# Norm rows from a broadcast column, and the residual added by an accumulating DMA, in a hybrid transformer layer

## The chip, the core and the metric

The kernel runs on one core of one Trainium2 chip. A core has a matrix engine (TensorE, PE in the profile, with its weight loads shown apart as PEld), three engines for element-wise work (VectorE or DVE, ScalarE or ACT, GpSimd or POOL), and SyncE (SP), which here only issues DMAs. Each engine works through its own queue in order, and so a waiting instruction holds up all that is queued behind it. PE reads its operands from the on-chip memory SBUF and writes its results to PSUM, from where DVE or ACT must take them. The metric is the device time of one execution in microseconds (us); the figure for a kernel is the median of several executions.

## The reference, cut to what matters

One layer on x of 1024 tokens by 1024 features, all in float32. Four blocks follow one another, each between two RMS norms, with the residual added after the second:

```
h = h + 0.5 * rmsnorm(swiglu(rmsnorm(h, ffn1_pre_g)), ffn1_post_g)
h = h + rmsnorm(hybrid_mixer(rmsnorm(h, mix_pre_g)), mix_post_g)
h = h + rmsnorm(memory_cross_attention(rmsnorm(h, xa_pre_g), rmsnorm(mem, mem_g)), xa_post_g)
h = h + 0.5 * rmsnorm(swiglu(rmsnorm(h, ffn2_pre_g)), ffn2_post_g)

def rmsnorm(x, g):
    return x * rsqrt(mean(x * x, axis=-1) + 1e-6) * g
```

The mixer joins 16 heads of stick-breaking attention with a Mamba-2 scan (SSD); cross-attention has 4 heads on 256 memory tokens; the feed-forwards have 2816 hidden features.

## The kernel before, in words

Activations lie transposed: features on the 128 partitions, tokens along the free axis. The residual stream h is eight feature tiles (d = 0 to 7) for each of two halves of 512 tokens (hh = 0, 1), so a tile is 128 x 512 float32, 256 KB. To keep float32 accuracy at the speed of the reduced-precision type float32r, each operand is split into a high and a low part (`split`, line 262, and `scaled_split`, line 268: the high part by a cast on ACT, the low part by a subtraction on DVE), and each product is made of three matmuls (`mm3`, line 277): high by high, high by low, low by high. Weights come in over SP's queue and are split on the way (`wtile`, line 174); weights that are needed twice are split once and their parts stored by DMAs on POOL's queue (`khi`, `klo`, line 194). The matrix products of the feed-forwards are done in seven products in place of eight (Strassen's way), `seven` (line 782) and `down_first` (line 1007).

The program is laid out for PE. Every matmul and transpose passes through `_pe` (line 100), which chains it to the one before, so PE's order is the order of the program. `_pe` also keeps a clock: it adds up a cost for each product, some 0.42 ns per column of 512-column products and 213 ns for float32r products of fewer than 256 columns (`mm`, line 130). Other work is entered in a list `later` with a due time on that clock and is issued by `run_later` (line 122) once PE's program has come that far. A norm's products can instead be floating and pinned at a time (`pinned`, line 144). Instructions issued from the list keep the program's order on their engines (`kp`).

A norm has two steps. `rms_cols` (line 317) takes the sum of squares over features: DVE and ACT add up the squares of the eight tiles into one tile `acc` (`sumsq`, line 374), eight small products with a column of 1/1024 bring the mean per token into a column of one bank (tokens on the partitions, four columns for 512 tokens), and ACT and DVE turn it into 1/sqrt. `rms_rows` (line 341) turns these four columns into one tile in which every partition holds the 512 factors as a row, since features lie on the partitions where the factor is to be applied. It splits the columns into `ch` and `cl` (lines 347 and 348), DVE multiplies an identity with each of them into 128 x 512 diagonal tiles (line 358, into `dg` and a low tile that shares its place with the row to be made), and PE sums each over the partitions by a product with a matrix of ones (line 367); ACT copies the result out (line 369). With `behind=True` the products are issued apart from the column's steps. Nineteen rows are made in all, one of them 256 wide.

`post` (line 407) is the second norm of a block, with the residual and the first norm of the next block. For a half it issues `cols` (the column), `rows` (the row), and for each d `apply`: DVE scales the tile F by gain and row (line 428), DVE adds the old h (line 432), POOL issues the store of the new h to memory (line 437), and ACT and DVE split it for the next block (lines 270 and 272 by `scaled_split`). `presum` squares the new tile, and at the end come the next norm's column and row (`tail`). The old h has been loaded for this by `resid` (line 396): eight DMAs on POOL's queue (line 403), each with a due time, into the places of `XL`, the low parts of the operands. There are six such post norms: two in the first feed-forward's down products (`down_first`, lines 1114 and 1136), two in the mixer's output (`mix_out`, lines 2074 and 2078), two in cross-attention (`xattn`, lines 2204 and 2241; the last is issued at once, without due times). The second feed-forward ends otherwise (`down_seven`, `rows_end`) and has its own use of `resid` (lines 1199 and 1200).

In cross-attention (line 2081), the steps of one slice (transposing the softmax values, products with the memory values, results split into the o tiles `oh` and `ol`) alternate with the next slice's scores and, merged by cost, with the projection of a later slice's queries. `place` (line 81) sets aside a given number of bytes per partition so that the tiles behind it lie elsewhere; line 2137 does this ahead of the transposed softmax values and the o tiles. The loads of the keys and values (line 2093) are on POOL's queue.

Here, in the kernel before, are the lines of the row product and of one part:

```
        def product():
            ps = self.norm_bank()
            for i, x in enumerate(parts):
                self.mm(ps[:, 0 : nb * P], self.onesr, x.rearrange("p a b -> p (a b)"), i == 0, i == 1)
```

Of the kernel before, what the change touches and what calls it, by code (L numbers as in the profile page):

```python
# [18 lines left out]
P = 128  # L19
S = 1024  # L20
H = 512
# [25 lines left out]
class Kern:  # L47
# [82 lines left out]
    def mm(self, out, lhsT, rhs, start, stop):  # L130
        n = 1
        for d in out.shape[1:]:
            n *= d
        dt = rhs.dtype
        cost = n * 0.422 * (4 if dt == F32 else 1)
        if dt == F32R and n < 256:
            cost = 213.0
        self._pe(self.nc.tensor.matmul(out, lhsT, rhs, start=start, stop=stop, skip_group_check=self.more), cost)  # L138
# [202 lines left out]
    def rms_rows(self, c, home, behind=False):  # L341

        nc = self.nc
        nb = c.shape[1]
        cs = self.t(self.tp, [P, 16], F32R, "cs", bufs=1)
        ch, cl = cs[:, 0:nb], cs[:, 4 : 4 + nb]
        self.kp(nc.vector.tensor_copy(ch, c))
        self.kp(nc.vector.tensor_tensor(out=cl, in0=c, in1=ch.bitcast(F32), op=ALU.subtract))
        dg = self.t(self.tp, [P, 4, P], F32R, "dg", bufs=1)
        if isinstance(home, tuple):  # L350
            pool, tag = home
            low = self.t(pool, [P, 4, P], F32R, tag, bufs=1)[:, 0:nb, :]
        else:
            low = dg[:, nb : 2 * nb, :]
        parts = dg[:, 0:nb, :], low
        for o, x in zip(parts, (ch, cl)):
            self.kp(
                nc.vector.tensor_tensor(
                    out=o, in0=self.ident[:, :].unsqueeze(1).to_broadcast([P, nb, P]),
                    in1=x.bitcast(F32).unsqueeze(2).to_broadcast([P, nb, P]), op=ALU.mult,  # L360
                )
            )

        def product():
            ps = self.norm_bank()
            for i, x in enumerate(parts):
                self.mm(ps[:, 0 : nb * P], self.onesr, x.rearrange("p a b -> p (a b)"), i == 0, i == 1)
            r = self.t(pool, [P, H], F32, tag, bufs=1) if isinstance(home, tuple) else home
            self.kp(nc.scalar.copy(r, ps[:, 0 : nb * P]))
            return r  # L370

        return product if behind else product()
# [34 lines left out]
    def post(self, hh, gname, r2, gnext=None, out=None, step=None, spread=True, pins=(23000, 28000), accs=None, tail=None, times=None):  # L407
# [17 lines left out]
        def apply(d):  # L425
# [6 lines left out]
            self.kp(nc.vector.tensor_tensor(out=F, in0=F, in1=self.XL[hh][d], op=ALU.add))  # L432
            if out is not None:
                nc.sync.dma_start(out=out[d], in_=F)
                return
# [4 lines left out]
        if out is None:  # L440
            self.h[hh] = [self.tc.dram_tile([P, H], F32, name=self.nm(f"h{hh}{d}")) for d in range(KT)]
# [8 lines left out]
        if step is None:  # L450
# [4 lines left out]
            for d in range(KT):  # L455
                apply(d)
# [6 lines left out]
        for d in range(KT):  # L463
            t = t3 + step * d
            q.append((t, lambda d=d: apply(d)))
            if out is None:
                q.append((t + 800, lambda d=d: presum(d)))
        if out is None:
            c2 = self.t(self.rp, [P, 4], F32, f"cpre{hh}", bufs=2)
            nxt = {}  # L470
            t1, t2 = tail or (t1 + 4000, t2 + 4000)
            self.posted = T0 + t + 900
            q.append((t + t1, lambda: self.rms_cols([accs2], c2)))
            if spread:
                def tail_rows():
                    nxt["r"] = self.rms_rows(c2[:, :], (self.rp, f"rpre{hh}"))
                    if "to" in nxt:
                        self.R[nxt["to"]] = nxt["r"]

                q.append((t + t2, tail_rows))  # L480
            self.next_norm = (nxt, c2)
# [525 lines left out]
    def down_first(self, sp, rw, wdn, act_d, gpost, gnext):  # L1007
# [98 lines left out]
        self.resid(0, 2700, 22000)  # L1106
# [7 lines left out]
        self.post(0, gpost, self.C[0], gnext, step=4700, accs=accs[0], times=(12000, 15500, 17500), tail=(5500, 9000))  # L1114
# [6 lines left out]
        self.resid(1, 2700, 10000)  # L1121
# [14 lines left out]
        self.post(1, gpost, self.C[1], gnext, step=2400, accs=accs[1], times=(4500, 9500, 11500), tail=(13500, 19000))  # L1136
# [854 lines left out]
    def mix_out(self):  # L1991
# [3 lines left out]
        with self.pools("mo", ["r", "a"], ["b"]) as (rp, sp, sp2, dnp):  # L1995
# [44 lines left out]
            self.resid(0, 5000, 12000)  # L2040
            self.run_all(self.first)
            for n, (hh, part) in enumerate(passes):
# [29 lines left out]
                if n == 1:  # L2072
                    self.run_later(float("inf"))
                    self.post(0, "mix_post_g", None, "xa_pre_g", step=5000, spread=False, tail=(18000, 0))
                    self.resid(1, 5000, 17000)
                if n == 3:
                    self.flush(0)
                    self.post(1, "mix_post_g", None, "xa_pre_g", step=3000, spread=False, tail=(22000, 0))


    def xattn(self):
# [3 lines left out]
        with self.pools("xf", ["a", "b"], []) as (sp, sp2, pp):  # L2085
# [158 lines left out]
    def run(self):  # L2244
        nc, tc, ap = self.nc, self.tc, self.ap
        with tc.tile_pool(name="const", bufs=1) as cp, tc.tile_pool(name="state", bufs=1, reuse_waits="tile") as xp, \
# [14 lines left out]
            self.ident = self.t(cp, [P, P], F32, "ident")  # L2261
# [161 lines left out]
```

## Time and profile before

| | |
|---|---|
| time, median of 3 executions | 2641.63 us (2639.55 to 2644.81) |
| the profiled execution | 2645.18 us, its span 2643.4 us |
| granted TensorE clock, mean | 0.992 |
| idle time of PE over the span | 66.5 us |
| DMA | 528.87 MB, mean 200 GB/s |

The profile is of one execution. Its page gives the busy time of each engine; idle time of an engine that is not the bottleneck costs nothing by itself. Matmuls are pipelined, so a matmul's own duration (some 390 ns for 512 columns) is longer than the step from one start to the next (some 0.23 us). A line of the trace names the engine, the line of the kernel that issued the instruction (for products mostly that of a helper, 138), the operation, and the tiles as output, an arrow, and inputs; the buffer's number is left out. "xN" is the count. In the view of waits a line gives the waiting instruction, who released it, the total time in us, the number of times and the longest. In the view of windows each engine has its busy time in that stretch and the number of its instructions, and then follow the granted clock of TensorE as a share of the full one, the DMA engines' busy share and their GB/s. In the view of one line of code, durations are given as minimum, median and maximum in ns, and for DMAs the time from issue to landing in us. In the timeline a row begins with its start in us from the span's beginning and its length, and ends in brackets with the idle time of the engine before it and what ended it.

By stages, in us from the span's start: first feed-forward to about 690, SSD to about 1030, attention to about 1610 (the first output products begin within it), mixer output to about 1740, cross-attention to about 1980, second feed-forward to the end.

### The profile page before, as it was taken

To read this page: it belongs to the slowest core of one execution; us is meant where nothing else is said; L and a number is where in the kernel's file an instruction comes from. 1 tells how busy PE (TensorE), PEld (TensorE's weight loads), DVE (VectorE), ACT (ScalarE), POOL (GpSimd) and SP (SyncE) were. 2 spreads that over 40 slices of the span, in tenths; PEclk is the share of its full clock that TensorE was granted. 3 is DMA by queue.
4 is the path that set the end of the run, shared out by engine and by line. 5 is a ranking of instruction groups with operands and counts; after the bars stand their busy time and mean duration, and the time that the engine had idled before them with its cause. 6 is when DMAs were issued, how large, how long until landed. Compare 5 with 4: busy or idle time off the path is not lost.

```text
span 2643.4 us, 36454 instructions
## 1 busy us (share of the span) xinstructions
PE 2576.9 (97%) x12598; PEld 2135.0 (81%) x12598; DVE 1983.2 (75%) x3085; ACT 1262.9 (48%) x2276; POOL 530.8 (20%) x660
## 2 busy tenths in 40 slices
PE   8999999999999999999999998999999999999998
PEld 6788888887777778888888787887878788888887
DVE  7888787888678774777777777775448989895675
ACT  7544443545367783445554445254445433333432
POOL 1555552001100000000000001122012555542000
PEclk9999999999999999999999999999999999999999
DMA  5688887754721226433434458777667455555976
GB/s 209 238 308 302 304 282 252 255 193 158 259 79 45 71 70 196 115 99 108 109 108 115 146 178 323 252 274 252 218 230 272 167 187 203 195 180 210 347 276 218
DMA packets 225241, 528.87 MB, mean 200 GB/s; under 512 B 28064, under 2 KB 35104, under 8 KB 225056
## 3 DMA queue, kind: packets, MB, share of 16 engines
q1 hardware_dynamic: 190432, 419.56, 48.2%
q0 software_dynamic: 27424, 93.87, 9.8%
q10 hardware_dynamic: 7200, 13.11, 1.3%
q8 instruction: 99, 1.62, 0.3%
q14 instruction: 86, 0.70, 0.1%
HBM read 353.41 MB, written 152.04 MB: 191 GB/s over the span
## 4 chain that ended last, share of the span: by engine, by line
PE 79%; DVE 9%; DMA 6%; ACT 3%; issue 2%; POOL 1%; SPq 0%; DVEq 0%; ACTq 0%; POOLq 0%
PE mm L138 45%; PE dn L138 24%; PE z L138 2%; PE ms L138 2%; PE tr L141 2%; PE y L138 1%; PE ms L141 1%; DMA wraw<-act 1%; DMA raw<-act 1%; DVE hl L265 1%; DVE wlo L265 1%; PE seg L138 1%; DMA blk<-h 1%; DVE whi L265 0%; DMA oraw<-mix 0%
## 5 line engine op out<-in xcount | busy, mean ns | idle before, releaser
L138 PE MATMUL mm<-xh,whi 128*128 128x512 f32 x1288 | 511.5, 406 | 11.1 <-ACT xh L270 7.0
L138 PE MATMUL mm<-xh,wlo 128*128 128x512 f32 x1240 | 478.5, 393 | 3.2 <-DVE wlo L265 2.9
L138 PE MATMUL mm<-xl,whi 128*128 128x512 f32 x1188 | 467.8, 394 | 1.0 <-DVE xl L265 0.7
L138 PEld LDWEIGHTS mm<-xh,whi 128*128 128x128 f32 x1288 | 244.1, 189 | 53.6 <-ACT xh L270 6.9
L138 PEld LDWEIGHTS mm<-xh,wlo 128*128 128x128 f32 x1240 | 234.3, 189 | 55.3 <-DVE wlo L265 3.4
L138 PEld LDWEIGHTS mm<-xl,whi 128*128 128x128 f32 x1188 | 225.6, 190 | 34.1 <-DVE xl L265 1.8
L1823 DVE TENSOR_TENSOR_SCAN nb<-nb,begin 128x128 f32<-128x128 f32 (+7 forms) x128 | 171.7, 1352 | 55.0 <-ACT nb L1819 54.4
L1819 ACT ACTIVATE nb<-z,scale 128x128 f32<-128x128 f32 (+2 forms) x192 | 107.8, 580 | 88.8 <-PE z L138 87.7
L263 ACT CAST whi<-wraw 128x1024 fp32r<-128x1024 f32 (+1 forms) x89 | 81.2, 914 | 69.1 <-PE mm L138 39.1
L1856 POOL MEMSET ath<- 128x128 f32 x64 | 13.1, 205 | 499.0 <-PE mm L138 499.0
L265 DVE TENSOR_TENSOR wlo<-wraw,whi 128x1024 fp32r<-128x1024 f32 x61 | 74.4, 1220 | 38.3 <-ACT whi L263 38.0
L138 PE MATMUL dn<-xh,wlo 128*128 128x512 f32 x296 | 101.0, 389 | 0.0
L737 POOL TENSOR_TENSOR wc<-wraw,raw 128x512 f32<-128x512 f32 x57 | 87.5, 1535 | 66.6 <-DVE whi L265 30.7
L737 POOL TENSOR_TENSOR wc<-raw,wraw 128x512 f32<-128x512 f32 x55 | 85.5, 1555 | 66.5 <-DVE wlo L265 31.4
L819 POOL TENSOR_TENSOR ft<-ft,e 128x512 f32<-128x512 f32 x38 | 62.4, 1642 | 144.2 <-DVE e L818 85.7
L650 ACT ACTIVATE ft<-ft 128x512 f32<-128x512 f32 x88 | 55.4, 631 | 75.0 <-DVE ft L649 70.3
L263 ACT CAST ath<-tr 128x512 fp32r<-128x512 f32 (+1 forms) x107 | 58.2, 545 | 67.5 <-PE tr L141 66.1
L138 PE MATMUL dn<-xh,blk 128*128 128x512 f32 x280 | 90.2, 389 | 0.0
L265 DVE TENSOR_TENSOR atl<-tr,ath 128x512 fp32r<-128x512 f32 (+1 forms) x107 | 67.0, 629 | 29.2 <-ACT ath L263 28.9
L138 PE MATMUL dn<-xh,whi 128*128 128x512 f32 x256 | 88.0, 389 | 0.0
L138 PE MATMUL mm<-ath,v 128*128 128x256 f32 x320 | 86.2, 291 | 0.6 <-DVE sq L1838 0.6
L382 DVE TENSOR_TENSOR acc<-acc,sq 128x512 f32<-128x512 f32 x78 | 52.3, 684 | 42.5 <-ACT sq L381 42.2
(586 smaller groups left out, 6667.9 us busy)
## 6 DMA issues: line engine op xcount, KB each, us to landing
whi<-dwhi SPq DMA_DIRECT2D x57, 512.0 KB, 3.4
wlo<-dwlo SPq DMA_DIRECT2D x57, 512.0 KB, 4.2
wraw<-act SPq DMA_DIRECT2D x102, 256.0 KB, 4.4
raw<-act SPq DMA_DIRECT2D x96, 256.0 KB, 4.3
wraw<-in_w_gu SPq DMA_DIRECT2D x44, 512.0 KB, 4.4
raw<-in_w_gu SPq DMA_DIRECT2D x38, 512.0 KB, 4.8
khi<-whi POOLq DMA_DIRECT2D x30, 512.0 KB, 4.6
klo<-wlo POOLq DMA_DIRECT2D x30, 512.0 KB, 6.7
```

Of the source, the lines that this page charges most:

```text
L138: self._pe(self.nc.tensor.matmul(out, lhsT, rhs, start=start, stop=stop, skip_group_check=self.more), cost)
L141: self._pe(self.nc.tensor.transpose(out, src, self.ident if ident is None else ident), 109.0)
L263: self.kp(self.nc.scalar.copy(hi, src))
L265: (eng or self.nc.vector).tensor_tensor(out=lo, in0=src, in1=hi.bitcast(F32), op=ALU.subtract)
L382: self.kp(nc.vector.tensor_tensor(out=accs[i % 2], in0=accs[i % 2], in1=sq, op=ALU.add))
L650: nc.scalar.activation(t, t, AF.Silu)
L737: nc.gpsimd.tensor_tensor(out=t, in0=a, in1=b, op=op)
L819: nc.gpsimd.tensor_tensor(out=t1, in0=t1, in1=e, op=ALU.mult)
L1819: nc.scalar.activation(nb[:, s0:s1], z[:, 0:n], AF.Sigmoid, scale=sc[:, i : i + 1])
L1823: nc.vector.tensor_tensor_scan(out=nb[:, 0:Wd][:, ::-1], data0=nb[:, 0:Wd][:, ::-1], data1=begin[:, S - Wd : S][:, ::-1], initial=0.0, op0 ...
L1856: nc.gpsimd.memset(x[:, 0, :].bitcast(F32), 0.0)
```

## The change

Four edits, as the diff has them:

- The row product has no diagonal tiles any more. The four columns themselves, each broadcast along the free axis, are the weights of products with the identity as the moving operand, 128 columns each; two (high and low) for each of four columns, eight in all, each with a cost of 80 on the planner's clock. The identity tile is now of type float32r, and its float32 view serves the transposes.
- `post` no longer uses loaded copies of h. The part is divided: `scale` (the DVE scaling, then a DMA on POOL's queue that adds the old h from memory into F), and `lag` later `apply` (the store of the new h, the split). The loads by `resid` ahead of the six post norms are gone; the second feed-forward keeps its own.
- The due times change: in the first feed-forward, first half, column, row and first part go from 12000, 15500, 17500 to 16500, 18500, 20500, the step from 4700 to 3700, and the next norm from 5500 and 9000 behind the last part to 3500 and 6500; in the others so that the last `apply` falls due at about the same time as before.
- The place ahead of the o tiles in cross-attention grows from 128 to 384 bytes per partition.

```diff
-        dg = self.t(self.tp, [P, 4, P], F32R, "dg", bufs=1)
-        if isinstance(home, tuple):
-            pool, tag = home
-            low = self.t(pool, [P, 4, P], F32R, tag, bufs=1)[:, 0:nb, :]
-        else:
-            low = dg[:, nb : 2 * nb, :]
-        parts = dg[:, 0:nb, :], low
-        for o, x in zip(parts, (ch, cl)):
-            self.kp(
-                nc.vector.tensor_tensor(
-                    out=o, in0=self.ident[:, :].unsqueeze(1).to_broadcast([P, nb, P]),
-                    in1=x.bitcast(F32).unsqueeze(2).to_broadcast([P, nb, P]), op=ALU.mult,
-                )
-            )
+        pool, tag = home if isinstance(home, tuple) else (None, None)
 
         def product():
             ps = self.norm_bank()
-            for i, x in enumerate(parts):
-                self.mm(ps[:, 0 : nb * P], self.onesr, x.rearrange("p a b -> p (a b)"), i == 0, i == 1)
-            r = self.t(pool, [P, H], F32, tag, bufs=1) if isinstance(home, tuple) else home
+            for b in range(nb):
+                for i, x in enumerate((ch, cl)):
+                    self.mm(
+                        ps[:, b * P : (b + 1) * P], x[:, b : b + 1].to_broadcast([P, P]), self.identr,
+                        i == 0, i == 1, 80.0,
+                    )
+            r = self.t(pool, [P, H], F32, tag, bufs=1) if pool else home
...
+        before = self.h[hh]
+
+        def scale(d):
             F = self.F[hh][d]
             self.kp(
                 nc.vector.scalar_tensor_tensor(
                     out=F, in0=F, scalar=self.par(gname, d), in1=box["r"], op0=ALU.mult, op1=ALU.mult
                 )
             )
-            self.kp(nc.vector.tensor_tensor(out=F, in0=F, in1=self.XL[hh][d], op=ALU.add))
...
+            self.kp(nc.gpsimd.dma_start(out=F, in_=before[d], accum_op=ALU.add))
+
+        def apply(d):
+            F = self.F[hh][d]
             self.XL[hh][d] = self.xl(hh, F32R)
             self.kp(nc.gpsimd.dma_start(out=self.h[hh][d], in_=F))
             self.scaled_split(self.XH[hh][d], self.XL[hh][d], F, self.par(gnext, d))
...
+            for d in range(KT):
+                scale(d)
             for d in range(KT):
                 apply(d)
...
+            q.append((t, lambda d=d: scale(d)))
+            q.append((t + lag, lambda d=d: apply(d)))
+            q.append((t + lag + 800, lambda d=d: presum(d)))
...
-        self.resid(0, 2700, 22000)
...
-        self.post(0, gpost, self.C[0], gnext, step=4700, accs=accs[0], times=(12000, 15500, 17500), tail=(5500, 9000))
+        self.post(0, gpost, self.C[0], gnext, step=3700, lag=4000, accs=accs[0], times=(16500, 18500, 20500), tail=(3500, 6500))
...
-        self.resid(1, 2700, 10000)
...
-        self.post(1, gpost, self.C[1], gnext, step=2400, accs=accs[1], times=(4500, 9500, 11500), tail=(13500, 19000))
+        self.post(1, gpost, self.C[1], gnext, step=2400, lag=4000, accs=accs[1], times=(4500, 8500, 10500), tail=(10500, 15500))
...
-            self.resid(0, 5000, 12000)
...
-                    self.post(0, "mix_post_g", None, "xa_pre_g", step=5000, spread=False, tail=(18000, 0))
-                    self.resid(1, 5000, 17000)
+                    self.post(0, "mix_post_g", None, "xa_pre_g", step=4500, spread=False, tail=(18000, 0))
...
-                    self.post(1, "mix_post_g", None, "xa_pre_g", step=3000, spread=False, tail=(22000, 0))
+                    self.post(1, "mix_post_g", None, "xa_pre_g", step=2600, spread=False, tail=(21500, 0))
...
-                    self.place(sp, 128)
+                    self.place(sp, 384)
...
-                if s == 2:
-                    self.resid(0, 4000)
...
-                    self.post(0, "xa_post_g", None, "ffn2_pre_g", step=5000, times=(8000, 15500, 18500))
+                    self.post(0, "xa_post_g", None, "ffn2_pre_g", step=4500, times=(8000, 15500, 18500))
...
-                if s == 6:
-                    self.resid(1, 4000)
...
-            self.ident = self.t(cp, [P, P], F32, "ident")
+            self.identr = self.t(cp, [P, P], F32R, "ident")
+            self.ident = self.identr.bitcast(F32)
...
-                nc.scalar.copy(self.ident, cst[:, 0, :])
+                nc.scalar.copy(self.identr, cst[:, 0, :])
```

`lag` is 3500 where a call doesn't name it.

More of the change, by code (lines that the diff above doesn't have):

```diff
@@ L128, in run_later, with mm @@
         self.inlater = False
-    def mm(self, out, lhsT, rhs, start, stop):
+    def mm(self, out, lhsT, rhs, start, stop, cost=None):
         n = 1
@@ L134, in mm @@
         dt = rhs.dtype
-        cost = n * 0.422 * (4 if dt == F32 else 1)
-        if dt == F32R and n < 256:
-            cost = 213.0
+        if cost is None:
+            cost = n * 0.422 * (4 if dt == F32 else 1)
+            if dt == F32R and n < 256:
+                cost = 213.0
         self._pe(self.nc.tensor.matmul(out, lhsT, rhs, start=start, stop=stop, skip_group_check=self.more), cost)
@@ L405, in resid, with post @@
         self.later += [(self.clock + start + step * d, lambda d=d: one(d)) for d in range(KT)]
-    def post(self, hh, gname, r2, gnext=None, out=None, step=None, spread=True, pins=(23000, 28000), accs=None, tail=None, times=None):
+    def post(self, hh, gname, r2, gnext, step=None, lag=3500, spread=True, pins=(23000, 28000), accs=None, tail=None, times=None):
         nc = self.nc
@@ L423, in rows @@
             box["r"] = self.rms_rows(c, (self.fp, "rpost"))
-        def apply(d):
+        before = self.h[hh]
+        def scale(d):
             F = self.F[hh][d]
@@ L438, in apply @@
             self.scaled_split(self.XH[hh][d], self.XL[hh][d], F, self.par(gnext, d))
-        if out is None:
-            self.h[hh] = [self.tc.dram_tile([P, H], F32, name=self.nm(f"h{hh}{d}")) for d in range(KT)]
+        self.h[hh] = [self.tc.dram_tile([P, H], F32, name=self.nm(f"h{hh}{d}")) for d in range(KT)]
         accs2 = []
```

32 lines of the change are left out of this document (13 added, 19 removed).

## The prediction

> **What bounds the kernel now.** I read the page first, for the busy shares.
>
> ```profile
> span 2643.4 us, 36454 instructions
> PE 2576.9 (97%) x12598; PEld 2135.0 (81%) x12598; DVE 1983.2 (75%) x3085; ACT 1262.9 (48%) x2276; POOL 530.8 (20%) x660
> ```
>
> TensorE (PE) is the bound: outside its busy time lie 2643.4 - 2576.9 = 66.5 us. A change that touches only VectorE (DVE) work and DMAs can win no more than PE's waits and what follows from them. So the next view is the list of waits, for PE alone; these are its rows that belong to norms.
>
> ```profile
> PE dn L138 <- DVE acc L384: 4.7, 1, 4.7
> PE ms L138 <- DVE rpre L358: 4.4, 2, 3.8
> PE ms L138 <- DVE dg L358: 3.3, 3, 2.3
> PE ms L138 <- DVE acc L384: 2.5, 1, 2.5
> PE ms L138 <- DVE atl L265: 1.9, 1, 1.9
> PE mm L138 <- DVE ft L649: 1.4, 1, 1.4
> PE dn L138 <- DVE dg L358: 0.9, 1, 0.9
> ```
>
> Together 19.1 us: over a quarter of PE's idle time stands at a handful of norms. `acc` is a sum of squares that the column products read, `dg` and the low half (`rpre` here) are the diagonal tiles that the row products read. The third view is the table of windows, laid over the stretches where the granted clock is down (the clock is the third number from the end; the first busy time is PE's).
>
> ```profile
> 613.50:620.30 6.80, 6.23 (x19) 5.26 (x20) 6.80 (x12) 3.76 (x6) 0.00 (x0) 0.50 0.39 114
> 668.10:674.90 6.80, 6.59 (x20) 5.53 (x21) 4.49 (x12) 1.94 (x4) 2.00 (x4) 0.50 0.89 308
> 1483.90:1494.10 10.20, 6.38 (x18) 4.96 (x19) 5.19 (x9) 3.71 (x7) 0.00 (x0) 0.50 0.51 142
> 1613.60:1617.00 3.40, 3.40 (x10) 2.62 (x9) 3.17 (x8) 1.22 (x2) 0.00 (x0) 0.50 1.03 418
> ```
>
> Each of the four lies at one of those waits, and the clock is at half. Half of PE's busy time in it is lost: 3.1, 3.3, 3.2 and 1.7 us. With the waits, norms cost some 30 us, 1.1% of the span. That is the most that this change can take out; about 0.2% (5.3 us) is what a measurement of this kernel can tell from no change.
>
> **Part 1, the norm rows.** Removed are the diagonal tiles:
>
> ```profile
> L358 DVE TENSOR_TENSOR dg<-ident,cs x20: 417/684/693, 26.8 to 2014.5; 128x512 fp32r<-128x512 f32 x18, 128x256 fp32r<-128x256 f32 x2
> L358 DVE TENSOR_TENSOR rpre<-ident,cs x8: 674/684/686, 27.4 to 2015.1; 128x512 fp32r<-128x512 f32 x8
> L358 DVE TENSOR_TENSOR rpost<-ident,cs x6: 682/684/685, 622.6 to 1983.3; 128x512 fp32r<-128x512 f32 x6
> L358 DVE TENSOR_TENSOR rn<-ident,cs x4: 680/682/685, 1612.5 to 1701.6; 128x512 fp32r<-128x512 f32 x4
> ```
>
> 38 instructions for 19 rows: 36 x 0.684 + 2 x 0.417 = 25.5 us of DVE, and 1.4 us off the way from a column to its row. Added is PE work: 8 products of 128 columns in place of 2 of 512. The nearest rows are two row products, and two products of the same type with 128 columns and weights of their own:
>
> ```profile
> 1471.87 0.39 PE L138 MATMUL ms<-dg,onesr 128*128 128x512 f32 x1
> 1472.10 0.39 PE L138 MATMUL ms<-rpre,onesr 128*128 128x512 f32 x1
> ...
> 1477.22 0.22 PE L138 MATMUL z<-k,q 128*128 128x128 f32 x1
> 1477.28 0.28 PE L138 MATMUL z<-k,ql 128*128 128x128 f32 x1
> 1477.39 0.44 PE L138 MATMUL mm<-xh,whi 128*128 128x512 f32 x1
> ```
>
> From start to start the wide ones take 0.23 us, a pair 0.46; the narrow ones 0.06 and 0.11. Eight cost 0.48 to 0.88 us, so a row costs 0.02 to 0.42 us more, 18 wide rows 0.4 to 7.6 us. I take 0.075 each, nearer to the step between two of a kind: 0.6 - 0.46 = 0.14, times 18 = +2.5 us. The Trainium skill (TensorE: Matmul & The Clock Gate, Back-to-back issue gap) gives about 81 ns for a steady stream of weight loads and 128-column products; by it the term would be 18 x (0.65 - 0.46) = +3.4 us, inside the bounds.
>
> What the shorter way wins I go through wait by wait.
>
> (a) Attention, the second row of the mixer norms:
>
> ```profile
> 1483.84 0.80 PE L138 MATMUL ms<-dg,onesr 128*128 128x512 f32 x1 [1.90 <-DVE atl L265]
> 1486.37 0.69 DVE L1719 TENSOR_TENSOR ev<-mm,rpre 128x512 f32<-128x512 f32 x1
> 1487.71 0.68 DVE L358 TENSOR_TENSOR rpre<-ident,cs 128x512 fp32r<-128x512 f32 x1
> 1488.45 0.79 PE L138 MATMUL ms<-rpre,onesr 128*128 128x512 f32 x1 [3.81 <-DVE rpre L358]
> ```
>
> The low half is written into the tile of the old row, which L1719 still reads at 1486.37; PE, between its two products, waits 3.8 us for it. After the change nothing but the ScalarE copy writes that tile, and PE goes on. The 1.9 us before it are a wait for the shared bank; they stay, and with them one stretch of half clock (the shortest seen is 3.4 us, 1.7 lost). Gain 3.8 + 3.2 - 1.6 = 5.4; bounds 3.8 and 8.9.
>
> (b) First feed-forward, first norm. The column products move 4.5 us later, to where `acc` is ready, so the 4.7 us go. But the rows now follow 2.0 us after them (3.5 before), and DVE is behind there:
>
> ```profile
> 614.07 1.87 PE L138 MATMUL dn<-small,acc 128*128 128x1 f32 x8 [4.70 <-DVE acc L384]
> ...
> 619.96 0.68 DVE L265 TENSOR_TENSOR whi<-bh,whi 128x512 fp32r<-128x512 f32 x1
> 620.56 0.15 DVE L332 TENSOR_TENSOR cpost<-dn,cpre 128x4 f32<-128x4 f32 x1
> ```
>
> The products end at 615.9; DVE turns to their result 4.6 us later, with weight splits back to back before it. PE would meet that lag at the rows instead. Ends: a gain of all 4.7 + 0.9 + 3.1 = 8.7, or a loss of some 3 if PE stands about 8 us at the rows (4.7 + 4.6 less 2.0, and the column's own steps). What speaks for a gain: eight loads of 256 KB leave this stretch. I take +3.
>
> (c) The next norm, at 668: 2.5 us for `acc`, 0.6 of the `rpre` row, 3.3 of clock = 6.4 us. It comes at the end of eight `apply` steps, each of which loses a DVE addition (part 2). Against it: the columns are planned 2 us nearer to the last `apply`, which now waits for a DMA. I take 4; bounds 0 and 6.4.
>
> (d) At 1612.7 PE waits 2.3 us for `dg`; one diagonal of 0.68 us stood between column and product. Gain 1; bounds 0.7 and 4.0 (2.3 and the clock's 1.7). (e) At the start of the kernel and elsewhere: 1.4 us for `ft`, which waits for the first row, and the last 1.0 of the `dg` row. Gain 2; bounds 0.5 and 2.4.
>
> Gains together: 5.4 + 3 + 4 + 1 + 2 = 15.4 us.
>
> **Part 2, the residual.** Six post norms have eight parts each. Removed per part: a POOL load of h and a DVE addition; added: a POOL DMA that adds h into F, `lag` (3.5 or 4.0 us) ahead of the cast.
>
> The scaling that stays, as the view by lines has it, and then the removed addition and who waits for it (the other 8 of 48 carry another tile's name):
>
> ```profile
> L428 DVE SCALAR_TENSOR_TENSOR F<-F,params,rpost 128x512 f32<-128x512 f32 x40 | 29.3, 743 | 3.6 <-ACT rpost L369 3.6
> ```
>
> ```profile
> L432 DVE TENSOR_TENSOR F<-F,xl x40: 669/683/694, 626.2 to 2003.1; 128x512 f32<-128x512 f32 x40
> ...
>   POOL h L437: 225.8, 34
>   ACT xh L270: 72.1, 31
> ```
>
> DVE is freed of 48 x 0.683 = 32.8 us; with part 1 it falls to about 1925 us. That is cover, not path: it is worth what (c) already counts. The number of DMAs stays; each now sits between the scaling and the cast. An accumulating DMA is not in this trace. The nearest rows are the loads of h, here of line 403 from 1760 to 1880 us and from 1880 to 2000 us:
>
> ```profile
> DMA to landing us min/median/max: 3.8/7.8/8.4
> ...
> DMA to landing us min/median/max: 3.1/4.2/7.6
> ```
>
> An addition reads F besides, so I don't assume it faster than a load; without the bursts in which the loads are issued now it needn't be slower either. I take these medians, 7.8 and 4.2 us, with the fastest, 3.1, and twice the slower median as bounds.
>
> So ScalarE's cast comes late by 0.74 (scaling) + landing - 3.5: 5.0 us in the mixer's second post norm, 1.4 us in cross-attention's first. On ACT, behind the waiting cast, stand softmax exponentials and splits that PE needs; on DVE the low half, and behind it the evacuations; on POOL the store of h now waits for the landing, and behind it the stores of split weights (they free weight buffers), the loads of k and v, and the next part's addition. In the first feed-forward and in the mixer's first post norm PE works from operands split several products ahead and hides this. In cross-attention it has less cover:
>
> ```profile
> 1740.00:1790.00 50.00, 47.69 (x250) 40.18 (x248) 43.76 (x98) 30.57 (x62) 10.73 (x20) 1.00 0.86 305
> 1900.00:1945.00 45.00, 42.29 (x218) 34.67 (x219) 36.22 (x85) 24.73 (x57) 10.14 (x19) 1.00 0.59 195
> ```
>
> PE idles 2.3 and 2.7 us there, although ACT already waits 2.3 us on average before a cast (72.1 us in 31 times). The added waits are 8 x 5.0 + 8 x 1.4 = 51 us of ACT; ends are 0 and a third of it, 17 us, on PE. I take 4 us, because waits of the present size cost so little.
>
> **Edits with one answer.** The planner's cost of 80 for a narrow product moves later events by 0.2 us a row, nothing. The identity as a reduced-precision tile has the same bytes. The o tiles move by 256 bytes a partition:
>
> ```profile
> L138 PE MATMUL dn<-xh,blk 128*128 128x512 f32 x280 | 90.2, 389 | 0.0
> L138 PE MATMUL mm<-oh,whi 128*128 128x512 f32 x128 | 50.2, 392 | 0.2 <-ACT oh L263 0.2
> ```
>
> A product from them lasts 392 ns against 389, so 384 products can win or lose about 1 us; I take 0. SP's queue has nothing moved on it, and the last feed-forward keeps its loads.
>
> **Sum.** -15.4 + 2.5 + 4 = -8.9 us. The profiled execution took 2645.2 us (span 2643.4 and 1.8 around it), 3.6 above the median of 2641.6; from it 2636.3, against the median 2632.7.
>
> **Rivals.** *Waits change places* (chance 0.21): DVE's lag meets PE at the rows in (b) and the accumulation holds up (c), so both give nothing: -5.4 - 1 - 2 + 6.5 = -1.9, 2639.7 us. For it: DVE back to back from 614 to 620 us; against it: the loads and additions that leave.
>
> *The additions reach PE in cross-attention* (0.19), the slower end. A third of the 51 us of ACT waits stops PE, and two stretches of half clock (3.4 us each, 1.7 lost) follow: 17 + 3.4 = 20.4 in place of my 4, net +7.5, 2649.1 us. It decides from the point where PE loses more than 15.4 - 2.5 = 12.9 us, a quarter of these waits. For it: landings of 7.8 us against a lag of 3.5; against it: the 2.3 us average that PE bears now.
>
> *Everything lands in time* (0.20): (b) and (c) in full and no wait for an addition: -5.4 - 8.7 - 6.4 - 1 - 2 + 2.5 = -21.0, 2620.6 us. It needs landings under 2.8 us; in the rows the fastest load of h took 3.1. The Trainium skill (DMA: Bandwidth & Descriptors, Anatomy of one DMA) puts a POOL DMA at about 2.0 us and its bytes at 436 GB/s, 2.6 us for 256 KB, which would be in time; the landings above, from 3.1 us up, disagree with it.
>
> **How the numbers follow.** My case, 2628 to 2637, has 0.40. Faster by over 0.2% (under 2636.3) is my case and the fast rival: 0.60; within 0.2% the rival of places: 0.21; slower the third: 0.19. The range takes in most of the fast rival and reaches the slow one's 2649: 2617 to 2649.
>
> **What would show it.** No `dg` and no L432 addition; DVE near 1925 us; the 3.8 us wait at the attention's last row gone; half-clock stretches at 613 and 668 gone or short; a wait of PE at the first feed-forward's rows if (b) is wrong; ACT's waits before L270 now ended by a DMA, 1 to 5 us each; PE busy within 1740:1790 and 1900:1945 no more than some 4 us lower in all. I'm wrong if the narrow products start over 0.11 us apart, if an addition lands well beyond 8 us, or if the wait at 1484 stays.

## The result, and the profile after

The changed kernel takes 2700.45 us (2694.03 to 2703.2, six executions) against 2641.48 us (2638.8 to 2644.81, six executions) for the kernel before, measured with it: ratio 1.0218, 95% interval 1.0204 to 1.0233. It is 59 us slower, where 8.9 us faster was forecast. The profiled execution has this page:

```profile
span 2699.7 us, 36566 instructions
...
PE 2602.4 (96%) x12708; PEld 2155.9 (80%) x12708; DVE 1934.2 (72%) x2999; ACT 1263.5 (47%) x2276; POOL 550.3 (20%) x660
```

VectorE did fall, by 49.0 us (58.3 were forecast), and the kernel is slower all the same: outside PE's busy time lie 97.3 us now in place of 66.5, and PE's busy time itself grew by 25.5 us. The view of waits for PE alone says who made it idle (in the changed kernel products have line 139 or, as transposes, 142; the cast is line 271, the low half behind it 273, the scaling 422, the accumulating DMA 426, the store of h 431):

```profile
PE ms L139 <- DVE acc L376: 15.5, 3, 9.9
PE mm L139 <- ACT xh L271: 8.9, 2, 7.6
PE dn L139 <- ACT pt L264: 8.3, 3, 4.2
PE dn L139 <- DVE sq L1981: 6.3, 2, 5.1
PE ms L139 <- DVE asum L2002: 5.3, 1, 5.3
PE mm L139 <- DVE zs L1269: 4.3, 1, 4.3
...
PE dn L139 <- ACT qh L264: 3.3, 1, 3.3
...
PE ms L139 <- DVE atl L266: 1.7, 1, 1.7
...
PE dn L139 <- DVE cs L348: 1.2, 1, 1.2
```

The `rpre` and `dg` rows are gone, `atl` stayed (1.7 us, 1.9 before). But new names stand at the top: sums of squares, softmax parts, evacuations. Only `acc` and `xh` depend on a tile that an addition writes (7.6 us of `xh` are the kernel's first product, 7.0 before); the rest is other work of VectorE and ScalarE. The view of windows over the new stretches of half clock, and over the two cross-attention stretches of the forecast, moved with the work (the first busy time is PE's, the clock is third from the end):

```profile
660.90:674.55 13.65, 7.68 (x22) 6.30 (x23) 6.76 (x12) 3.64 (x6) 1.60 (x3) 0.50 0.36 138
1695.10:1701.90 6.80, 6.10 (x14) 4.78 (x15) 4.82 (x9) 1.24 (x2) 1.44 (x2) 0.50 0.41 78
...
2060.30:2070.50 10.20, 6.97 (x21) 5.84 (x22) 6.21 (x9) 4.43 (x7) 5.99 (x9) 0.50 0.88 317
1769.00:1819.00 50.00, 45.72 (x226) 37.79 (x225) 31.02 (x70) 23.05 (x46) 16.99 (x26) 0.93 0.98 310
1941.00:1986.00 45.00, 37.97 (x176) 29.68 (x175) 26.81 (x68) 20.17 (x47) 9.90 (x15) 0.92 0.57 146
```

In the last two PE idles 4.3 and 7.0 us where it idled 2.3 and 2.7, and VectorE does 31.0 and 26.8 us of work where it did 43.8 and 36.2: it does 12.7 and 9.4 us less, where eight additions taken off it are 5.5 us, so other work of VectorE has been put off too. The view of line 426 gives the additions' own times (issue in ns as minimum, median and maximum, here of 24 of the 48; who waited, in us and times, and the landing in us, of all 48):

```profile
L426 POOL DMA_DIRECT2D F<-h x24: 876/898/1848, 1778.0 to 2039.0; - x24
...
  ACT xh L271: 143.2, 44
  POOL h L431: 119.2, 38
...
DMA to landing us min/median/max: 3.6/5.1/17.5
```

And the view of the cast's line names who waits behind the cast. First the kernel before, then the changed one:

```profile
  DVE xl L272: 15.5, 19
```

```profile
  DVE xl L273: 113.5, 44
```

ScalarE's wait before its casts doubled, from 72 to 143 us. VectorE's wait behind them grew sevenfold, by 98 us. How this reaches PE shows in the timeline of the mixer's output, for one part:

```profile
1683.28 0.75 DVE L273 SCALAR_TENSOR_TENSOR xl<-xl,params,xh 128x512 fp32r<-128x512 f32 x1 [5.46 <-ACT xh L271]
1683.95 0.74 DVE L422 SCALAR_TENSOR_TENSOR xl<-xl,params,rpost 128x512 f32<-128x512 f32 x1
...
1685.00 0.88 POOL L426 DMA_DIRECT2D xl<-h  x1 [1.65 <-DVE xl L422]
...
1692.37 0.72 ACT L271 ACTIVATE xh<-xl,params 128x512 fp32r<-128x512 f32 x1 [8.60 <-DMA xl<-h]
...
1693.13 0.75 DVE L273 SCALAR_TENSOR_TENSOR xl<-xl,params,xh 128x512 fp32r<-128x512 f32 x1 [7.83 <-ACT xh L271]
...
1694.40 0.74 DVE L422 SCALAR_TENSOR_TENSOR xl<-xl,params,rpost 128x512 f32<-128x512 f32 x1
1695.06 0.68 DVE L1981 TENSOR_TENSOR sq<-dn,rn 128x512 f32<-128x512 f32 x1
...
1695.80 0.79 PE L139 MATMUL dn<-xh,whi 128*128 128x512 f32 x1 [5.11 <-DVE sq L1981]
```

The addition is issued at 1685.0 and has landed at 1692.4, the slowest of this norm's eight (their median is 4.3 us). ScalarE stood 8.6 us for it; VectorE, next in the chain with the low half, stood 7.8 us; behind the low half in VectorE's queue was L1981, which takes a finished product out of PSUM. PE waited 5.1 us for L1981 and began at half clock (the second window above).

The same rows show why a landing of 4.3 us can hold up a cast that has a lag of 3.5 us. In this norm a part begins every 4.5 us of the list, later than the lag, so in VectorE's order the scaling of a part (L422) stands behind the low half of the part before (L273, at 1683.28 and 1693.13). The parts therefore go one after the other, each with a whole landing in it: the first seven scalings of this norm start 8.2 us apart on average, against 4.9 us in the run without additions below.

### The profile page after: what moved, and what is told of

Read it like the earlier page. It is cut to its first block, busy times and chain, and to the rows that moved or that the text cites. A ratio compares the mean times of both kernels' runs of the same rounds, so it can differ in the third digit from the quotient of the medians.

```text
span 2699.7 us, 36566 instructions
## 1 busy us (share of the span) xinstructions
PE 2602.4 (96%) x12708; PEld 2155.9 (80%) x12708; DVE 1934.2 (72%) x2999; ACT 1263.5 (47%) x2276; POOL 550.3 (20%) x660
## 4 chain that ended last, share of the span: by engine, by line
PE 73%; DMA 9%; DVE 9%; issue 5%; ACT 3%; POOL 1%; SPq 0%; DVEq 0%; ACTq 0%; POOLq 0%
PE mm L139 41%; PE dn L139 23%; PE z L139 2%; DMA F<-h 2%; PE ms L139 2%; DMA F<-in_xT 2%; PE tr L142 1%; PE y L139 1%; DMA wraw<-act 1%; PE ms L142 1%; DMA xl<-h 1%; DVE hl L266 1%; PE seg L139 1%; DVE wlo L266 1%; DMA raw<-act 1%
## 5 line engine op out<-in xcount | busy, mean ns | idle before, releaser
L273 DVE SCALAR_TENSOR_TENSOR xl<-F,params,xh 128x512 fp32r<-128x512 f32 x40 | 30.0, 750 | 75.4 <-ACT xh L271 75.4
```

Of the source, the lines that this page charges most:

```text
L273: self.nc.vector.scalar_tensor_tensor(out=lo, in0=src, scalar=g, in1=hi.bitcast(F32), op0=ALU.mult, op1=ALU.subtract)
```

## The experiments

Theory A, formed on these views: the cast, and on VectorE the low half behind it, stand until the addition has landed; the loss goes by how much longer the landing takes than the list leaves between scaling and cast. Theory B: the narrow row products cost PE far more than was taken. Later rivals stand with their runs. All times are medians. Each ratio is to the kernel before, timed again with the run: 2640.38 us for the first four runs below; 2639.27 for "Kind or place", "Additions where they fit", "The due times alone" and "The o tiles"; 2640.77 for "The last norm by itself", "Off the chain" and "The add on GpSimd".

**The narrow rows alone**, on the kernel before: the diff's first part and the float32r identity, nothing else.

> The kernel before with the narrow row products alone (no diagonal tiles), everything else as before. Theory A (the casts and, behind them, VectorE stand still until an accumulating DMA has landed, longer than the lag): this kernel has no such DMA, so it is faster than before, 2630 to 2638 us, the 3.8 us wait at the attention's last row gone. Theory B (the narrow products cost TensorE far more than 0.14 us a row, or hold it up): 2655 us or more.

Measured: 2631.59 us, ratio 0.9968 (0.9958 to 0.9978), faster by 8.8 us. Theory B falls.

**The reverse**: the changed kernel with the diagonal tiles back.

> The changed kernel with the diagonal tiles and wide row products of before put back; accumulating DMAs, due times and place as changed. Theory A: the loss stays, 2695 to 2712 us, and the waits of ScalarE before the cast of line 271's kind sum up to over 100 us. Theory B: most of the loss is gone, 2640 to 2655 us.

Measured: 2710.91 us, ratio 1.0268 (1.0251 to 1.0285), in theory A's range; ScalarE's casts wait 152 us for the additions. The whole loss is in the additions and the due times; the rows are worth some 10 us beside them too.

**No addition at all**, as a floor.

```diff
-            self.kp(nc.gpsimd.dma_start(out=F, in_=before[d], accum_op=ALU.add))
```

> The changed kernel without the accumulating DMAs; it leaves out that the old h is added in the six post norms, nothing else. The tile is ready for the cast when VectorE has scaled it. Theory A: all the new waits go, 2612 to 2630 us. Theory B (narrow products, due times or the moved o tiles): 2680 us or more.

Measured: 2624.29 us, ratio 0.9939 (0.9920 to 0.9957), as theory A had it. The additions cost 76 us in the changed kernel. Its page:

```profile
span 2623.1 us, 36480 instructions
...
PE 2572.9 (98%) x12708; PEld 2136.8 (81%) x12708; DVE 1930.6 (74%) x2999; ACT 1262.5 (48%) x2276; POOL 506.2 (19%) x612
```

PE has the same 12708 products here. So of the 76.6 us between the two spans, 97.3 - 50.2 = 47.1 are waits and 2602.4 - 2572.9 = 29.5 are products run at half clock.

**A longer lag**: 9 us between scaling and cast in the five norms with a list, the tails moved so that the ends stay.

```diff
-        self.post(0, gpost, self.C[0], gnext, step=3700, lag=4000, accs=accs[0], times=(16500, 18500, 20500), tail=(3500, 6500))
+        self.post(0, gpost, self.C[0], gnext, step=3000, lag=9000, accs=accs[0], times=(16500, 18500, 20500), tail=(3500, 6500))
...
-                    self.post(0, "xa_post_g", None, "ffn2_pre_g", step=4500, times=(8000, 15500, 18500))
+                    self.post(0, "xa_post_g", None, "ffn2_pre_g", step=4500, lag=9000, times=(8000, 15500, 18500))
```

> The changed kernel with the accumulating DMAs, but apply 9.0 us behind scale in place of 3.5 or 4.0 (step 3.0 in place of 3.7 in the first post norm, so that its last part falls due as before; the next norms' due times kept where that can be). Most landings took 3.6 to 8 us from issue, so a cast finds its tile landed. Theory A: 2620 to 2645 us, all but the last post norm, which has no lag, is mended. If the additions hurt by their load on the DMA queues rather than by the order, it stays near 2690.

Measured: 2653.65 us, ratio 1.0046 (1.0031 to 1.0061): 47 of the 76 us come back. That is far from the 2690 us of the rival and 9 us above theory A's range: the waits for additions are most of the loss, and more was left than theory A allowed. The longer lag also changes the order, since 9 us are longer than a step, so that one scaling or more runs ahead of the cast that waits; no run tells the two apart. The largest single rest is the last post norm, which has no list and no lag:

```profile
2005.00:2035.00 30.00, 24.54 (x102) 20.31 (x101) 22.36 (x32) 14.83 (x24) 10.34 (x16) 0.83 0.87 310
```

The stages make this finer. For each trace I took the starts of the same products (the first of the feed-forward's down products, of the SSD's state products, of the mixer's output, of cross-attention's scores, the last of its output, the last `mm<-S,blk`), and give how much longer each stretch is than without any addition, in us; traces differ by 2 or 3 us in a stretch without any edit. What lies ahead of the first of these products and behind the last (-1.9 to 2.5 us) is left out.

| kernel | first ffn's end | SSD, attention | mixer output | cross-attention | last post norm and on |
|---|---|---|---|---|---|
| before | 8.3 | 5.0 | -0.1 | 5.7 | 2.2 |
| changed | 20.8 | -1.1 | 19.0 | 24.7 | 10.5 |
| narrow rows alone | 4.9 | -0.7 | -0.2 | 1.1 | 2.1 |
| lag 9 us | -0.1 | -0.9 | 4.5 | 8.7 | 10.5 |
| plain load, below | 10.7 | -0.7 | 12.7 | 14.9 | 4.4 |
| behind the cast, below | -1.2 | -2.1 | -0.6 | 12.1 | 16.8 |
| lag 9 us, last norm as before, below | -0.2 | 0.6 | 7.1 | 9.4 | 0.5 |

**The last norm by itself**: the lag of 9 us, and loads and VectorE adds in the last post norm alone.

> The changed kernel with 9 us between scale and cast, and the old loads and VectorE adds in the last post norm alone (the one with no list, whose eight additions are issued back to back). If what is left of the loss after the longer lag is mostly that queue of eight: the wait of TensorE for the squares near 2010 us (5.5 us, and 10.2 us at half clock) is gone and the time is 2643 us (2640 to 2647). If it lies in the waits of the cross-attention at 1780 us and later: 2650 us or more.

Measured: 2642.64 us, ratio 1.0003 (0.9993 to 1.0012), 11 us less, as expected. In place of a wait of 5.5 us for the squares, PE is busy through the same place, at full clock:

```profile
1995.00:2025.00 30.00, 30.00 (x141) 24.93 (x141) 23.60 (x35) 14.57 (x22) 11.43 (x18) 1.00 0.94 330
```

**Kind or place**: the accumulating DMA made a plain load into the same tile.

```diff
-            self.kp(nc.gpsimd.dma_start(out=F, in_=before[d], accum_op=ALU.add))
+            self.kp(nc.gpsimd.dma_start(out=F, in_=before[d]))
```

> The changed kernel with each accumulating DMA made a plain load of h into the same tile, at the same place in the queue and behind the same scale. Leaves out the norm's output in the six post norms (F becomes the old h). Theory A (it is the place: a transfer of any kind between a scale and its cast): landing about 4 to 5 us as before, waits of ScalarE's casts over 100 us, time 2690 us (2680 to 2702). Theory B (it is the kind: reading F, adding and writing it back makes the transfer late): landing falls to about 2.8 us, the casts wait little, time 2640 us or less.

Measured: 2669.36 us, ratio 1.0111 (1.0094 to 1.0128). Both theories missed the number. The view of its line 426:

```profile
L426 POOL DMA_DIRECT2D F<-h x24: 536/538/548, 1763.2 to 2014.4; - x24
...
  ACT xh L271: 107.4, 36
...
DMA to landing us min/median/max: 2.8/4.2/8.5
```

A plain load at this place costs 2669.36 - 2624.29 = 45 us, with a median landing of 4.2 us; that it accumulates costs the other 31. Place is the larger part, but kind is no small one.

**Off the chain**: the same additions and stores (40 in the five norms with a list, 8 in the last), issued behind the cast, the low half and the sum of squares.

> The changed kernel with all its accumulating DMAs and stores of h, but issued behind the cast, the low half and the sum of squares of their tile and not ahead of them. Leaves out the old h in what the next stage multiplies and in the next norm's sums; h itself is still added and stored. Theory A (the loss is the wait of the cast, and what stands behind it on ScalarE and VectorE, for a transfer in its chain): the same 40 transfers, off the chain, cost next to nothing, 2626 us (2623 to 2632) beside 2624.3 without them. Theory B (GpSimd's longer issues, its queue behind each addition, or the traffic itself slow the kernel): 2650 us or more.

Measured: 2656.39 us, ratio 1.0063 (1.0046 to 1.0080). The number is that of theory B, and the stages split it. In the first feed-forward and the mixer's output the additions off the chain cost nothing (-1.2 and -0.6): there the loss comes from their place ahead of the cast, and not from GpSimd or the traffic. In cross-attention 12.1 us remain: the loads of the memory values go behind the additions and stores on POOL's queue, and PE waits twice for one of them (4.9 and 3.3 us), which landed in 10.2 and 5.7 us where these loads took 3.6 to 4.2 us without additions. The last 16.8 us are this edit's own: the next block reads the new h from memory (`blk`), and here it is stored later. The waits of PE for the values, and of VectorE for the split of `blk`:

```profile
  PE dn L139: 8.2, 2
```

```profile
2020.75 0.69 DVE L672 TENSOR_TENSOR wc<-blk 128x512 f32<-128x512 f32 x1 [14.81 <-ACT blk L662]
```

**Additions where they fit**: narrow rows, additions with a lag of 9 us in the first feed-forward alone, loads and VectorE adds elsewhere.

> The narrow rows, with the accumulating DMAs in the first feed-forward alone, there with 9 us between a scale and its cast and with the moved due times; the mixer and the cross-attention keep their loads and VectorE adds. Theory A (a cast, and the VectorE low half behind it, stand until the addition has landed; what is lost goes by the time that the list leaves between the two): with 9 us nothing waits in this stage, the start of the mixer is reached 10 us before the kernel of before as in the run with 9 us everywhere, the two later stages run as with the narrow rows alone, so 2624 us (2620 to 2629). Theory B (an addition on its own costs TensorE time wherever it stands, by the queue of GpSimd or by the traffic): 2636 us or more.

Measured: 2631.30 us, ratio 0.9966 (0.9954 to 0.9978): 2 us above theory A's bound, 5 below theory B's. The stage itself is as A had it, 0.8 us longer than without additions; the trace loses 2.8 us ahead of it, where no edit is. What it shows beyond that: additions in time at the moved due times are worth no more than additions on VectorE at the old ones (2631.59, the narrow rows alone).

**The due times alone**: narrow rows, loads and adds kept, the first feed-forward's norms at the moved times.

> The narrow rows, the loads and VectorE adds kept everywhere, and the first feed-forward's norms at the moved due times (first product at 18.5 us of its list in place of 15.5, next norm's columns and rows 2 to 2.5 us nearer the last apply). If the 7 us that the version without any addition has over the narrow rows in this stage come from the moved times, 2626 us (2623 to 2629) and the wait before the first row near 613 us and the one at 667 us are gone; if they come from the additions taken off VectorE, 2631 us as with the rows alone (2629 to 2637, later if the nearer columns wait for the longer apply).

Measured: 2638.91 us, ratio 0.9996 (0.9985 to 1.0007): 7 us worse than with the old times: with the additions on VectorE the moved times bring nothing, and the nearer columns wait, as the second alternative put it, 2 us beyond its 2637. At the same moved times the additions by DMA with a lag of 9 us took 7.6 us less (2631.30), so there it is worth something that VectorE is rid of them and the loads are gone. (Its profiled execution, at 2631.93, was the fastest of ten.) That one too has the next norm's wait (5.0 us for `acc`) with half clock:

```profile
658.40:668.60 10.20, 7.24 (x21) 6.08 (x22) 5.50 (x10) 3.20 (x6) 2.34 (x5) 0.50 0.43 149
```

**The o tiles**: narrow rows, 384 in place of 128.

> The narrow rows alone with the o tiles moved (384 in place of 128). The forecast took the move at 0, plus or minus 1 us: 2631.6 us, as without it. A rival, that the move costs part of what the changed kernel loses in the cross-attention: over 2635 us, with new waits of TensorE between 1750 and 1980 us.

Measured: 2631.26 us, ratio 0.9970 (0.9960 to 0.9981). The move is worth nothing.

**The add on GpSimd**: narrow rows, loads kept, `nc.gpsimd.tensor_tensor` for the add in five norms, cast 3.5 or 4 us behind the scaling.

> The narrow rows, with the loads of h kept and the add made by GpSimd from on-chip memory in five of the six post norms, at the changed kernel's lags (3.5 and 4 us); the last norm adds on VectorE. GpSimd's adds of this size take 1.5 us in the trace of before, so a cast comes after 0.7 + 1.5 us, inside the lag. Theory A: nothing waits, and VectorE is rid of 28 us that were cover: 2630 us (2625 to 2633) beside 2631.6 with the adds on VectorE, 2624 if the 7 us that the version without any addition is ahead are VectorE's relief. Rival: GpSimd's queue is late with weight rounding and transfers, and casts wait as for the DMA: 2640 us or more.

Measured: 2641.17 us, ratio 1.0000 (0.9990 to 1.0009). The rival was right: 8 to 10 us are lost against the add on VectorE (by the ratios and by the medians), and casts wait for POOL where they waited for the DMA.

```profile
L425 POOL TENSOR_TENSOR F<-F,xl x32: 1270/1386/4070, 624.2 to 1938.6; 128x512 f32<-128x512 f32 x32
...
  ACT xh L271: 62.3, 29
```

VectorE's wait behind the casts is 24.7 us here, against 15.4 with the narrow rows alone and 113.5 in the changed kernel. How much of the 8 to 10 us comes through it isn't shown.

The best version found is the narrow rows without the rest, 2631.59 us. The two others within a microsecond of it carry more edits and no more gain.

## Why the prediction was wrong, step by step

**Part 1, the rows, was right in sign.** They give 8.8 us alone. (a) The 3.8 us wait went, the `atl` wait and one stretch of 3.4 us of half clock stayed in the run with the rows alone; the stretch from the SSD to attention's end is 5.0 + 0.7 = 5.7 us shorter, 5.4 were taken. (The forecast took off 1.6 us for that stretch, where its own row gives 1.7.) (b) In the changed kernel the 4.7 us wait became 1.2 at the rows, at full clock: 6.6 with the clock, where 3 was taken. (d) The wait for `dg` is gone; (e) that for `ft` fell to 0.7 us in the run with the rows alone and gave little.

The price of the products was wrong. Before, and with the narrow rows, the same row product in the timelines:

```profile
685.75 0.39 PE L138 MATMUL ms<-dg,onesr 128*128 128x512 f32 x1
685.98 0.39 PE L138 MATMUL ms<-rpost,onesr 128*128 128x512 f32 x1
686.21 0.39 PE L138 MATMUL mm<-xh,whi 128*128 128x512 f32 x1
```

```profile
682.95 1.00 PE L139 MATMUL ms<-ident,cs 128*128 128x128 f32 x8
683.79 0.45 PE L139 MATMUL mm<-xh,wlo 128*128 128x512 f32 x1
```

A row takes 0.84 us in place of 0.46, +0.38, times 18 = 6.8 us where 2.5 was taken: the upper bound's 0.11 a product was the truth, and the step of 0.06 between two products did not carry over. Each of these products has a weight load of its own, and around the pair that the forecast went by (1477.1 to 1477.4 us in the trace of before) the weight loads start 0.11 to 0.12 us apart: over a row of eight it is that step which came out. The Trainium skill's figure (TensorE: Matmul & The Clock Gate, Back-to-back issue gap) gives some 81 ns; the trace disagrees: eight in 0.84 us are 105 ns each.

**(c) failed**: a gain of 4 was taken, and PE stood 9.9 us at 667 with 13.65 us at half clock. The clause put against it, columns 2 us nearer to a last part that waits for a DMA, decided: the last addition, issued at 654.7, landed in 8.8 us, and its squares belong to `acc`. At the same due times PE waited under 1 us for `acc` without any addition and with a lag of 9 us, and 5.0 us with the additions on VectorE.

**Part 2 failed in its cover, not in the landings that it priced.** The step that failed is the +4 us of the sum, the price of the additions' waits on PE. It put the first feed-forward and the mixer's first post norm at nothing, cross-attention at 4 us, and had no term for the last post norm; the stages lost 20.8, 19.0, 24.7 and 10.5 us against the kernel without additions. The landings came out as taken where the forecast took any: 7.8 and 4.2 us were assumed for the mixer's second post norm and cross-attention's first, and the view of line 426 in these two windows says

```profile
DMA to landing us min/median/max: 4.1/7.5/8.7
...
DMA to landing us min/median/max: 4.0/4.5/5.6
```

Even plain loads, with a median of 4.2 us over all six norms, cost 45 us. Of the forecast's three signs of being wrong one came, a landing well beyond 8 us: 11.5 us in the first feed-forward and 17.5 in the last norm were the longest. Two sentences were wrong, and one place was left out.

"In the first feed-forward and in the mixer's first post norm PE works from operands split several products ahead and hides this": these stretches lost 20.8 and 19.0 us. Split operands were not what ran out. In the mixer's output it was VectorE's evacuations, which stood behind the low half (5.1 us in the timeline above). In the first feed-forward the longest wait, 9.9 us, was the next norm's column, which needs the last addition itself, as under (c); the next, 4.3 us, was again an evacuation by VectorE (`zs`, L1269), after VectorE had stood 8.9 us for a cast.

"I take 4 us, because waits of the present size cost so little": in the kernel before ScalarE waited 72 us before its casts because VectorE was at work on the same part; VectorE itself waited 15.5 us behind them. The wait that the change adds stops both at once. It had the same name in the view and another price. The formula for the cast's delay also took it that each scaling comes on time, 3.5 us ahead; in the mixer's first norm each came behind the part before it. The rival that put a third of those waits on PE in cross-attention had the right mechanism, with 17 us and 3.4 of clock; the stage lost 24.7.

"That is cover, not path" put VectorE's 32.8 us into (c), and no run shows them worth much more: without any addition, without the loads of h and at the moved due times the kernel is 7.3 us faster than with the narrow rows alone. But nothing was priced at the last post norm, where the eight additions are issued back to back. The view of line 426 in that window:

```profile
L426 POOL DMA_DIRECT2D F<-h x8: 876/1416/1848, 2033.5 to 2039.0; - x8
...
DMA to landing us min/median/max: 4.2/11.3/17.5
```

They share one queue. ScalarE's casts there each end on a landing; these are the first and the last of the eight:

```profile
2037.72 0.73 ACT L271 ACTIVATE xh<-F,params 128x512 fp32r<-128x512 f32 x1 [5.27 <-DMA F<-h]
...
2056.51 0.72 ACT L271 ACTIVATE xh<-F,params 128x512 fp32r<-128x512 f32 x1 [1.92 <-DMA F<-h]
```

Seven steps in 18.8 us: the additions land 2.7 us apart, and this place alone was worth 11 us.

Last, the clock. The slow rival added 3.4 us of lost clock to 17 us of waits. Measured were 29.5 us for 47.1. In the changed kernel's trace there are nine waits of PE between 3 and 10 us behind the start, spread over the kernel, and each brought a stretch of 3.4 to 13.7 us at half clock; of the shorter waits only some did.

**Right**: the o tiles at 0, and the wait at 1484 us, which went. Most of the 9 us that a lag of 9 us leaves in cross-attention lie at one place in its trace: an addition issued at 1770.6 lands in 7.6 us, ScalarE stands 4.9 us for it at a cast, the softmax exponential is behind the cast (1779.4), PE waits 4.7 us for what is made from it, and 6.8 us at half clock follow, in which half of PE's 4.05 busy us is lost: 4.7 + 2.0 = 6.7 us. Open: which part of the 11 us that the last norm cost is the additions' own transfer and which the later start of the next block's loads of h; and whether the lag's length or the order that it brings mended more.

## What to carry to other kernels

Before a transfer is put between two steps of an in-order chain, list what stands behind the second step on each engine, and ask which of it feeds the bottleneck; the wait costs by that too, even where the transferred tile itself isn't needed soon. A wait in the old profile is no measure for a new one of the same name: look whether the releaser was working or waiting too. Compare the lag with the step as well: where the lag is shorter, each part's first step queues behind the part before, and a transfer's whole time is paid part by part. And work taken off an engine that is not the bound bought some 7 us at most here, which couldn't pay for the 76 us that the new waits cost.

## What the runs showed of the hardware

- An accumulating DMA of 256 KB from memory into SBUF on POOL's queue took a median of 0.88 to 0.90 us to issue, a plain load at the same place 0.54; landing 3.6/5.1/17.5 us (minimum, median, maximum) against 2.8/4.2/8.5. Eight in a row landed 2.7 us apart, and the casts behind eight plain loads started 1.6 us apart.
- Products of 128 columns with weights of their own started 0.105 us apart, where one of 512 columns takes 0.23: a quarter of the columns cost nearly half of the time.
- Waits of PE were paid again in clock: against the run without additions, 0.63 us of slower products for each us of added waiting (29.5 to 47.1). In the changed kernel each of the nine waits of 3.3 to 9.9 us behind its start brought 3.4 to 13.7 us at half clock.
